# Attention: probabilities scaled on two engines and transposed by the identity

## The chip, the cores and the metric

The kernel runs on one core of a Trainium2 chip. A core has five engines that run side by side, each through its own queue of instructions in order: TensorE (PE in the profile; its weight loads are PEld), VectorE (DVE), ScalarE (ACT), GpSimd (POOL) and SyncE (SP), which issues the DMA transfers. Matrix products read SBUF and write PSUM, eight banks of 128 partitions by 512 float32 values. The metric is the device time of one execution in microseconds, the median of several.

## The reference, cut to what matters

The reference is a two-layer decoder trunk on 512 tokens of 1024 features in float32: a gated mixer, two gated feed-forward parts with a short convolution, per-layer embeddings, and, in the second layer, sliding-window attention with 16 heads of 64 features over 4 shared key and value heads. The change lies in the attention alone:

```python
scores = einsum('bnikgd,bnjkd->bnkgij', q, kblk) * (HEAD_DIM ** -0.5)
scores = scores - slopes * dist            # ALiBi
scores = where(valid, scores, -inf)        # this block of 128 keys and the one before
m = maximum(max(scores), sink)
e = exp(scores - m)
probs = e / (sum(e) + exp(sink - m))
out = einsum('bnkgij,bnjkd->bnikgd', probs, vblk)
out.reshape(B, S, 1024) @ w_o
```

## The kernel before, in words

Features lie on the 128 partitions and the 512 tokens along the free dimension. Every large product is made of three float32r products: weights and activations are each split into a rounded high part and a remainder (`wh`, `wl`; `xh`, `xl`), and high x high, high x low and low x high are added in PSUM (`mm3`, L162 to L170; `mm3t`, L172 to L181, for products with the tokens on the partitions). Weights stream in by DMA into raw buffers (`load`, L117, issued at L124), ScalarE casts the high part of each unit (L141) and VectorE subtracts for the low part (L142). The planned list of pieces is used in the order in which the layers need them. During the attention steps a single raw buffer is in use.

The attention (L622 to L720) takes 16 steps: four groups of four heads, and in each group four blocks of 128 tokens. The first block of a group sees 128 keys, the other three see 256. A step `i` passes through four functions, each written out for a different step in one pass of the loop: `scores(i)`, then filler work, `mix(i - 2)`, `turn(i - 1)` and `weights(i)`.

- `scores(i)`, L622: for each of the four heads, two products of queries and keys (L636, L637) into a half of a PSUM bank (tile `sc`). VectorE adds the position term, masks, writes the result to `pr` in SBUF and keeps the row's extreme in `neg` (L639). ScalarE takes the exponential in place and accumulates the sums `sm` (L644), and the exponential of the sink, `ds` (L648). `pr` has two buffers.
- `weights(i)`, L651: VectorE adds the sums to `ds` and takes the reciprocal (L654, L655), so that `ds` holds one factor per token and head. Then it builds `dg`, four 128 x 128 diagonal matrices with these factors (L657). `dg` has one buffer.
- `turn(i)`, L660: TensorE multiplies each 128 x 128 block of `pr` with its diagonal (L667). The block is the stationary operand, so the result in PSUM (tile `tr`) is the block transposed, with keys on the partitions, and scaled. `split` (L213) lets ScalarE write the rounded high part (L214) and VectorE the remainder (L215).
- `mix(i)`, L678: products with the values (L691) into `pv`, which ScalarE and VectorE split into the two parts of the attention output (`oh`, `ol`, L697 and L698).

The filler work of a step (`beside`, L593) is a piece of the projection of the next group's queries (tile `q`), of the values (`vv`) or, towards the end, of the output projection (`o`). Queries of groups 1 to 3 are scaled on VectorE (L529), split by ScalarE and VectorE (L540, L541) and moved by DMA from SP's queue into the two halves of the score operand (L544, L545).

A scheduler orders the instructions of each engine; `scores`, `turn` and `weights` stand under a higher priority, so that they are placed ahead of filler work that is ready at the same time. PSUM has eight banks, all shared by one pool.

Of the kernel before, what the change touches and what calls it, by code (L numbers as in the profile page):

```python
# [8 lines left out]
F32 = mybir.dt.float32  # L9
F32R = mybir.dt.float32r  # L10
AF = mybir.ActivationFunctionType
ALU = mybir.AluOpType

P = 128
# [11 lines left out]
GQ = HEADS // GROUPS  # L26
# [20 lines left out]
def tile_yoco(ctx: ExitStack, tc: tile.TileContext, t, out: bass.AP, out_b: bass.AP):  # L47
    nc = tc.nc
# [10 lines left out]
    def psum(name):  # L59
        return mmp.tile([P, S], F32, tag="mm", name=name)  # L60
# [144 lines left out]
    ident = const.tile([P, P], F32, name="ident")  # L205
# [7 lines left out]
    def split(src, hi, lo):  # L213
        nc.scalar.copy(hi, src)  # L214
        nc.vector.tensor_sub(lo, src, hi.bitcast(F32))  # L215
# [241 lines left out]
    for c in range(4):  # L457
# [4 lines left out]
        for j in range(2):  # L462
# [7 lines left out]
            for b in range(NC):  # L470
                nc.tensor.matmul(sp[:, b * P : (b + 1) * P], zv[b][:, m * P : (m + 1) * P], wsT[:, m, :],
                                 start=True, stop=True)
# [19 lines left out]
    at = ctx.enter_context(tc.tile_pool(name="at", bufs=1))  # L492
# [127 lines left out]
    live = {}  # L620
# [30 lines left out]
    def weights(i):  # L651

        pr, nk, sm, ds = live[i]
        nc.vector.tensor_add(ds, ds, sm)  # L654
        nc.vector.reciprocal(ds, ds)  # L655
        dg = at.tile([P, GQ, P], F32, tag="dg", name=f"dg{i}")
        nc.vector.tensor_mul(dg, ident.unsqueeze(1).to_broadcast([P, GQ, P]), ds.unsqueeze(2).to_broadcast([P, GQ, P]))  # L657
        live[i] = (pr, nk, dg)

    def turn(i):  # L660

        pr, nk, dg = live[i]
        pts = []
        for b in range(nk // P):
            tr = psum(f"tr{i}_{b}")
            for e in range(GQ):
                nc.tensor.matmul(tr[:, e * P : (e + 1) * P], pr[:, e, b * P : (b + 1) * P], dg[:, e, :],  # L667
                                 start=True, stop=True)
            q = state["pt"] = (state["pt"] + 1) % 3
            if q == 2:  # L670
                ph, pl = (ap.tile([P, S], F32R, tag=f"a{x}{SLOTS - 1}", name=f"p{x}{i}_{b}") for x in "hl")
            else:
                ph, pl = pts4[:, 2 * q, :], pts4[:, 2 * q + 1, :]
            split(tr, ph, pl)
            pts.append((ph, pl))
        live[i] = pts
# [27 lines left out]
    for i in range(last + 2):  # L704
        if i < last:
            with tc.high_priority():
                scores(i)
        fill(i)
        if i >= 2:
            mix(i - 2)  # L710
        if 0 <= i - 1 < last:
            with tc.high_priority():
                turn(i - 1)
        if i < last:
            with tc.high_priority():
                weights(i)
# [95 lines left out]
    for q in range(2):  # L812
        for c, ps in enumerate(turned):
            y = tp.tile([P, S], F32, tag=f"c{c}", name=f"y{c}_{q}")
            r = root[1][:, c : c + 1]
# [71 lines left out]
```

## Time and profile before

| | |
|---|---|
| median of 3 runs | 1176.94 us (1176.49 to 1177.97) |
| profiled execution | 1177.48 us, its span 1175.8 us |
| granted TensorE clock | 0.999 |
| PE busy | 1160.8 us, 99% |
| PEld busy | 989.0 us, 84% |
| DVE busy | 747.2 us, 64% |
| ACT busy | 521.0 us, 44% |
| POOL busy | 77.4 us, 7% |
| products with the diagonal (L667) | 224 instructions, from 605.4 to 713.2 us |
| diagonals (L657) | 16, 687 ns each |

The span runs from the first to the last instruction of the core. A row of a group names the line, the engine, the operation, the tile that is written and the tiles that are read, the partitions and elements, then how often it occurs, its busy time in total, the mean duration of one in ns, and the idle time of the engine ahead of it with what ended it. A row of the order in time has the start and the duration in us first. The durations of neighbouring products on TensorE overlap in these rows, because a product is shown from its start to the end of its pipeline; the distance between starts tells what one costs in a stream.

### The profile page before, as it was taken

Reading aid. Unit: us, or ns where it says so; the run is one execution under the profiler, and the core shown is the slowest. Engines: PE = TensorE matmul, PEld = TensorE weight load, DVE = VectorE, ACT = ScalarE, POOL = GpSimd, SP = SyncE. Lnnn points to the kernel's source line nnn. Section 1 sums busy time; section 2 is a strip of 40 time slices with the busy share of each in tenths; the row PEclk is TensorE's granted clock in tenths of the full one; section 3 lists DMA queues with packets and bytes.
Section 4 is the critical chain, followed back from the end, with each engine's and each line's share of the span. In section 5 each row is a group of like instructions: output and inputs, shape, how many; then the busy total and the mean of one; then the engine's idle time right before and its main releaser. Section 6 shows DMA issues by size and latency. Waiting matters only on the chain.

```text
span 1175.8 us, 14550 instructions
## 1 busy us (share of the span) xinstructions
PE 1160.8 (99%) x5830; PEld 989.0 (84%) x5830; DVE 747.2 (64%) x1159; ACT 521.0 (44%) x845; POOL 77.4 (7%) x87
## 2 busy tenths in 40 slices
PE   7999999999999999999999999999999999999997
PEld 7988888888888888888889888888888888888897
DVE  6365467763676377458877876577635773675665
ACT  5633444431344244545566665444313432345532
POOL 1000210000000000032100002100000000000221
PEclk9999999999999999999999999999999999999999
DMA  9232323322322333231243213322322233223302
GB/s 324 79 108 72 108 72 108 107 75 105 108 72 90 110 105 113 103 109 36 72 103 95 74 53 143 108 88 92 108 102 77 99 99 108 90 93 105 108 1 72
DMA packets 21570, 114.40 MB, mean 97 GB/s; under 512 B 2688, under 2 KB 4096, under 8 KB 11264
## 3 DMA queue, kind: packets, MB, share of 16 engines
q1 hardware_dynamic: 20672, 112.44, 28.3%
q8 instruction: 45, 0.74, 0.3%
q10 hardware_dynamic: 832, 1.05, 0.3%
q14 instruction: 21, 0.17, 0.0%
HBM read 107.19 MB, written 2.10 MB: 93 GB/s over the span
## 4 chain that ended last, share of the span: by engine, by line
PE 96%; DVE 1%; issue 1%; ACT 1%; DMA 0%; SPq 0%; POOLq 0%; POOL 0%; DVEq 0%; ACTq 0%
PE up L170 14%; PE up L168 14%; PE up L169 14%; PE d L169 8%; PE d L170 8%; PE d L168 8%; PE gate L169 2%; PE gate L168 2%; PE gate L170 2%; PE tr L667 2%; PE pv L691 1%; PE v L179 1%; PE v L180 1%; PE v L181 1%; PE o L170 1%; PE o L168 1%
## 5 line engine op out<-in xcount | busy, mean ns | idle before, releaser
L142 DVE TENSOR_TENSOR wl<-wraw,wh 128x1024 fp32r<-128x1024 f32 (+1 forms) x198 | 238.6, 1206 | 141.6 <-ACT wh L141 141.1
L141 ACT CAST wh<-wraw 128x1024 fp32r<-128x1024 f32 (+1 forms) x198 | 202.9, 1026 | 272.4 <-PE d L169 132.2
L168 PE MATMUL up<-nf10h,wh 128*128 128x512 f32 x352 | 137.1, 389 | 0.0
L168 PE MATMUL up<-nf00h,wh 128*128 128x512 f32 x352 | 137.1, 389 | 0.0
L170 PE MATMUL up<-nf00h,wl 128*128 128x512 f32 x352 | 137.0, 389 | 0.0
L170 PE MATMUL up<-nf10h,wl 128*128 128x512 f32 x352 | 137.0, 389 | 0.0
L169 PE MATMUL up<-nf00l,wh 128*128 128x512 f32 x352 | 136.9, 389 | 0.0
L169 PE MATMUL up<-nf10l,wh 128*128 128x512 f32 x352 | 136.9, 389 | 0.0
L168 PE MATMUL d<-ah,wh 128*128 128x512 f32 x352 | 136.9, 389 | 0.0
L169 PE MATMUL d<-al,wh 128*128 128x512 f32 x352 | 136.9, 389 | 0.0
L170 PE MATMUL d<-ah,wl 128*128 128x512 f32 x352 | 136.9, 389 | 0.0
L325 ACT ACTIVATE c<-hs,vec 128x512 f32<-128x512 f32 x88 | 71.3, 813 | 71.8 <-DVE hs L321 71.1
L326 DVE SCALAR_TENSOR_TENSOR c<-hs,vec,c 128x511 f32<-128x511 f32 x88 | 65.8, 748 | 34.2 <-ACT c L325 34.2
L301 DVE TENSOR_TENSOR h<-h,d 128x512 f32<-128x512 f32 x56 | 38.4, 686 | 73.7 <-PE d L170 73.7
L169 PEld LDWEIGHTS up<-nf00l,wh 128*128 128x128 f32 x352 | 66.1, 188 | 13.8
L168 PEld LDWEIGHTS up<-nf10h,wh 128*128 128x128 f32 x352 | 66.1, 188 | 13.8
L168 PEld LDWEIGHTS d<-ah,wh 128*128 128x128 f32 x352 | 66.1, 188 | 13.8
L169 PEld LDWEIGHTS d<-al,wh 128*128 128x128 f32 x352 | 66.1, 188 | 13.7
L169 PEld LDWEIGHTS up<-nf10l,wh 128*128 128x128 f32 x352 | 66.1, 188 | 13.7
L170 PEld LDWEIGHTS up<-nf00h,wl 128*128 128x128 f32 x352 | 66.1, 188 | 13.7
L168 PEld LDWEIGHTS up<-nf00h,wh 128*128 128x128 f32 x352 | 66.1, 188 | 13.7
L170 PEld LDWEIGHTS up<-nf10h,wl 128*128 128x128 f32 x352 | 66.1, 188 | 13.7
(291 smaller groups left out, 2163.8 us busy)
## 6 DMA issues: line engine op xcount, KB each, us to landing
wraw<-in_w_up SPq DMA_DIRECT2D x44, 1024.0 KB, 4.8
wraw<-in_w_down SPq DMA_DIRECT2D x16, 896.0 KB, 4.5
wraw<-in_w_down SPq DMA_DIRECT2D x8, 1024.0 KB, 4.8
wraw<-in_w_gate SPq DMA_DIRECT2D x8, 1024.0 KB, 4.8
wraw<-in_w_u SPq DMA_DIRECT2D x4, 1024.0 KB, 5.9
wraw<-in_w_out SPq DMA_DIRECT2D x4, 1024.0 KB, 5.3
wraw<-in_w_q SPq DMA_DIRECT2D x4, 1024.0 KB, 4.8
wraw<-in_w_o SPq DMA_DIRECT2D x4, 1024.0 KB, 5.0
```

Source lines behind the costliest of these rows:

```text
L141: nc.scalar.copy(wh[:, :n], src)
L142: nc.vector.tensor_sub(wl[:, :n], src, wh[:, :n].bitcast(F32))
L168: nc.tensor.matmul(ps, wh[:, a:b], xh, start=st, stop=False)
L169: nc.tensor.matmul(ps, wh[:, a:b], xl, start=False, stop=False)
L170: nc.tensor.matmul(ps, wl[:, a:b], xh, start=False, stop=en)
L179: nc.tensor.matmul(ps, xh[:, s], wh[:, a:b], start=st, stop=False)
L180: nc.tensor.matmul(ps, xl[:, s], wh[:, a:b], start=False, stop=False)
L181: nc.tensor.matmul(ps, xh[:, s], wl[:, a:b], start=False, stop=en)
L301: nc.vector.tensor_add(h[m], h[m], ps)
L325: nc.scalar.activation(c, hs, AF.Identity, bias=v("conv_b", l * 2 * NJ + col), scale=cw[2])
L326: nc.vector.scalar_tensor_tensor(c[:, 1:], hs[:, : S - 1], cw[1], c[:, 1:], op0=ALU.mult, op1=ALU.add)
L667: nc.tensor.matmul(tr[:, e * P : (e + 1) * P], pr[:, e, b * P : (b + 1) * P], dg[:, e, :], start=True, stop=True)
```

## The change

In `weights`, the diagonal matrices are gone. The factors are applied to the exponentials themselves, in place in `pr`: of the four heads, VectorE scales heads 0 and 2 and ScalarE heads 1 and 3, each over all keys of the step (128 or 256). In `turn`, the product with the diagonal becomes the transpose operation of TensorE, with the constant 128 x 128 identity as the other operand. `ident` exists in both kernels. The tile `dg` is no longer allocated. All else is the same text; the scheduler places the instructions of the attention steps anew.

```diff
         nc.vector.tensor_add(ds, ds, sm)
         nc.vector.reciprocal(ds, ds)
-        dg = at.tile([P, GQ, P], F32, tag="dg", name=f"dg{i}")
-        nc.vector.tensor_mul(dg, ident.unsqueeze(1).to_broadcast([P, GQ, P]), ds.unsqueeze(2).to_broadcast([P, GQ, P]))
-        live[i] = (pr, nk, dg)
+        for e in range(GQ):
+            a, r = pr[:, e, :nk], ds[:, e : e + 1]
+            if e in (1, 3):
+                nc.scalar.activation(a, a, AF.Copy, scale=r)
+            else:
+                nc.vector.tensor_scalar_mul(a, a, r)
+        live[i] = (pr, nk)
 
     def turn(i):
 
-        pr, nk, dg = live[i]
+        pr, nk = live[i]
         pts = []
         for b in range(nk // P):
             tr = psum(f"tr{i}_{b}")
             for e in range(GQ):
-                nc.tensor.matmul(tr[:, e * P : (e + 1) * P], pr[:, e, b * P : (b + 1) * P], dg[:, e, :],
-                                 start=True, stop=True)
+                nc.tensor.transpose(tr[:, e * P : (e + 1) * P], pr[:, e, b * P : (b + 1) * P], ident)
```

## The prediction

> **What bounds the kernel now.** I read the page first (engines, then the chain that ended last), then the busy time of each engine over the attention steps, then TensorE's order of instructions in a few of them, then the groups of instructions by shape.
>
> ```profile
> span 1175.8 us, 14550 instructions
> PE 1160.8 (99%) x5830; PEld 989.0 (84%) x5830; DVE 747.2 (64%) x1159; ACT 521.0 (44%) x845; POOL 77.4 (7%) x87
> ...
> PE 96%; DVE 1%; issue 1%; ACT 1%; DMA 0%; SPq 0%; POOLq 0%; POOL 0%; DVEq 0%; ACTq 0%
> ```
>
> TensorE carries 96% of the chain. A change is worth what it takes from TensorE's stream, less what it makes TensorE wait. The edit lies in the 16 attention steps, about 595 to 716 us. Busy time there, in stretches of four steps (columns: PE, PEld, DVE, ACT, POOL, granted clock, DMA share, GB/s):
>
> ```profile
> 606.00:633.04 27.04, 27.04 (x185) 24.62 (x184) 20.50 (x56) 16.15 (x45) 0.00 (x0) 1.00 0.42 118
> 633.04:660.10 27.06, 26.89 (x182) 24.00 (x180) 21.48 (x69) 17.58 (x56) 0.00 (x0) 1.00 0.28 79
> 660.10:687.18 27.08, 26.95 (x181) 24.05 (x180) 20.83 (x69) 18.47 (x56) 0.00 (x0) 1.00 0.29 79
> ```
>
> TensorE is full, VectorE at 76 to 79%, ScalarE at 60 to 68%. TensorE's own wait for VectorE in the whole stage is 0.2 us (scores for the read of their bank). So its instructions set the period, and the next limits are VectorE and ScalarE, some 20% below.
>
> The durations of single products overlap; what one costs is the distance between starts:
>
> ```profile
> 704.27 1.95 PE L667 MATMUL tr<-dg,pr 128*128 128x128 f32 x16
> 705.97 0.36 PE L691 MATMUL pv<-pl,vth 128*128 128x256 f32 x1
> 706.17 0.29 PE L691 MATMUL pv<-ph,vtl 128*128 128x256 f32 x1
> 706.29 0.28 PE L691 MATMUL pv<-ph,vth 128*128 128x256 f32 x1
> ...
> 1168.21 0.36 PE L767 MATMUL fms<-mean,facc 128*128 128x1 f32 x2
> 1168.44 0.36 PE L767 MATMUL fms<-mean,fsq 128*128 128x1 f32 x2
> 1168.66 1.14 PE L804 MATMUL ht<-dgain,h 128*128 128x128 f32 x8
> ```
>
> From 704.27 to 706.17 stand 16 products and one pv, which elsewhere takes 0.12 (706.17 to 706.29): 1.78 us for 16, 0.111 each. The code issues 8 there, so one f32 product runs as two instructions of 0.111, 0.222 us together. The f32 products with one moving column take as long (1168.21 to 1168.44, two in 0.23): at this size the weight load sets the pace, not the 128 columns.
>
> ```profile
> L667 PE MATMUL tr<-dg,pr 128*128 128x128 f32 x224 | 31.1, 275 | 0.0
> L657 DVE TENSOR_TENSOR dg<-ident,ds 128x512 f32<-128x512 f32 x16 | 11.0, 687 | 0.1
> L454 DVE TENSOR_SCALAR zv<-zv,vrt 128x1024 f32<-128x1024 f32 x4 | 2.7, 749 | 1.1 <-POOL vrt L270 1.1
> L772 DVE TENSOR_SCALAR dgain<-ident,vec 128x128 f32<-128x128 f32 x8 | 1.7, 280 | 3.1 <-PE pin L169 3.1
> L644 ACT ACTIVATE pr<-pr,neg 128x256 f32<-128x256 f32 x48 | 24.3, 506 | 10.7 <-DVE neg L639 10.6
> L644 ACT ACTIVATE pr<-pr,neg 128x128 f32<-128x128 f32 x16 | 6.4, 400 | 5.5 <-DVE neg L639 5.4
> L570 ACT ACTIVATE vth<-vv,n1rt 128x256 fp32r<-128x256 f32 x4 | 1.9, 474 | 1.7 <-PE vv L181 1.5
> L697 ACT CAST oh<-pv 128x128 fp32r<-128x128 f32 x32 | 8.2, 257 | 3.6 <-DVE ol L698 1.9 <-PE pv L691 1.2
> ```
>
> **The change, part by part.**
>
> *TensorE.* 224 instructions are 112 products with the diagonal (12 steps of 8, 4 of 4), 24.9 us of the stream. The compiled program of the changed kernel holds 5718 matmuls and as many weight loads, 112 fewer than the 5830 of the page: a transpose is one pair, not two. No row shows a transpose. Bounds of its cost: no f32 instruction here, not even one of one column, follows another in less than 0.111; from above, what both passes take now, 0.222, or, if neighbours do not overlap, the 0.275 that one instruction lasts. I take 0.111, because probabilities are still the 128-column f32 weights whose load sets that pace. Gain 112 x 0.111 = **12.4 us**, all on the path; a stretch of four steps holds 28 products and shrinks from 27.1 to 24.0 us.
>
> The Trainium skill ("TensorE: Matmul & The Clock Gate", Terms) says that the transpose mode is four times faster for f32. By that rule a product would go from 0.222 to 0.056 and the gain would be 18.6 us; the one-column rows above speak for the load's 0.111 as the floor instead (rival D).
>
> *VectorE.* Loses 16 diagonals, 11.0 us. Gains two scalings a step, 24 of 128x256 and 8 of 128x128. No row has 128x256; between 280 ns (128 columns) and 749 (1024), both VectorE scalings of SBUF, a straight line gives 347 (bounds: 280, and 476 of the score read of 256 columns). 24 x 0.347 + 8 x 0.280 = 10.6 us. Net -0.4 (-2.0 to +2.7); its stretch stays near 21 us of 24.0, 86 to 89%. Off the path. The diagonal's single buffer also goes, so the scaling no longer waits for the previous step's products; it stands straight behind the reciprocal in nearly every step.
>
> *ScalarE.* Gains the other 32 scalings. For 256 columns the nearest row is the scaled copy of vth, 474 ns (bounds: 417, a Square of 256 columns, and 506, the exponential); for 128 columns 257 to 400, I take 330. 24 x 0.474 + 8 x 0.330 = 14.0 us, 3.5 a stretch: 21.1 and 22.0 us of 24.0, 88 to 92%. No further table load: seven in both programs.
>
> *The new wait.* ScalarE's scalings wait for VectorE's sum and reciprocal: at step 1 the sink's exponential starts at 602.44 and the reciprocal ends at 603.04, so 0.4 us after the exponential. In the changed order nothing stands between the two on ScalarE at steps 1, 2 and 12; elsewhere a copy of values or pv, or other casts do. Behind the waiting instruction are queued the casts of the transposed blocks, the query copies and the next exponentials; their readers are VectorE, SP and TensorE. TensorE needs a step's scaled block only a step later: from the end of a diagonal to its first product are 2.7 us or more, except 0.75 and 1.0 at steps 13 and 14. VectorE's half now comes earlier than the diagonal did, ScalarE's half about 1 us after the reciprocal, so this hides, with up to 0.5 us at step 14 where the cover is thin.
>
> *What is late next.* Queries of group 3 are first read by the second pair of scores of step 12. Their last half leaves VectorE after the last score read of step 11:
>
> ```profile
> 678.39 0.69 DVE L541 TENSOR_TENSOR qf<-qf,qhi 128x512 fp32r<-128x512 f32 x1
> ...
> 679.11 1.10 SPq L545 DMA_DIRECT2D q<-qf  x2
> ...
> q<-qf SPq DMA_DIRECT2D x12, 128.0 KB, 2.3
> ```
>
> The scores of step 11 end with the pair at 677.55, and the copy lands at 679.11 + 2.3 = 681.4, 3.9 us later; now TensorE comes for it at 681.8. In the changed order 1 pv, 5 transposes, 2 scores, 3 transposes, 10 pv, 2 scores and 1 pv stand between: 12 x 0.12 + 8 x 0.111 + three pairs of scores at 0.24 (the one of 677.55 with them) = 3.1 us. So TensorE waits 0.8 us there (0 to 1.3). At step 8 the same count gives 4.2 us, no wait. SP: the second and third w_o load now stand ahead of the copies of a group's second query projection instead of among them; they wait for the same casts as before, and the row of 2.3 was taken with such a load (1 MB, 5.0 us to landing) around it, so nothing (0 to 1 us). POOL is not touched.
>
> *Sum.* 1177.48 (profiled execution: span 1175.8 and 1.7 around it) - 12.4 + 0.8 (queries) + 0.7 (score reads: TensorE's next start is 0.3 late now at 655.80 in step 8 and at 682.89 in step 12; I let both double and round up for step 14) = 1166.6. The profiled execution lies 0.5 above the median of 1176.94, so **1166.0 us**.
>
> **Rivals.**
>
> *A. ScalarE or VectorE becomes the bound.* With the dearer prices ScalarE's stretch is 18.5 + 6 x 0.506 + 2 x 0.400 = 22.3, and with 0.6 us of wait for the reciprocal in each of four steps 24.7, over TensorE's 24.0. It decides once scalings and waits pass 5.5 us a stretch. Four stretches lose 0.7 each, and as much again through VectorE behind ScalarE's casts: 5.6 us, about 1171; 1169 to 1174.5. For it: 90% on two in-order engines that wait for each other. Against: one step of slack.
>
> *B. The transpose keeps the pace of both passes.* At 0.222 nothing is saved, ScalarE has 27 us for its 22: 1177, no change. For it: the 0.111 of the pass itself could be hidden under the load. Against: half the loads are gone.
>
> *C. Slower: transposes do not overlap.* Each takes the 275 ns of the L667 row: 112 x 0.275 = 30.8 against 24.9, +5.9, about 1183. It decides above 0.222 a product. For it: no row shows a transpose beside other products. Against: every f32 and fp32r product here overlaps its neighbour.
>
> The Trainium skill ("TensorE: Matmul & The Clock Gate", Part 4) gives about 275 ns for a transpose within one kernel.
>
> *D. A transpose takes a quarter of the f32 product*, 0.056, load included: 112 x 0.166 = 18.6, less 1.5 of waits, 1160. Against: no weight load here follows another so closely.
>
> *E. The clock falls around the transposes.* Half clock for 1 us of work in each of 16 steps costs 16 us: 1166 + 16 = 1182 or more. Against: the granted clock is 1.00 in all stretches, and transposes would fill 0.9 of some 6 us a step. The same Part 4 of the Trainium skill's "TensorE: Matmul & The Clock Gate" says that transposes do not count as busy for the clock gate; no run here shows it.
>
> **How the numbers follow.** Forecast (1163.5 to 1168.5) 0.66, A 0.10, B 0.09, C 0.10, D 0.04, E 0.01. Faster: forecast, A, D, 0.80. 0.2% is 2.4 us, about what a measurement of this kernel can tell from no change: B splits into same 0.07 and slower 0.02; with C and E slower is 0.13. The range takes in D and A: 1159.5 to 1174.5, 0.80.
>
> **What would show it.** TensorE's tr group: 112 instructions, starts 0.111 apart (B: 0.222, C: 0.275, D: 0.056). A stretch of four steps near 24.4 us. ScalarE's scalings near 0.47, VectorE's near 0.35. A wait for the query copy before the second pair of scores in step 12. The stages outside unchanged to 0.5 us. I am wrong if the distance between transposes is not 0.111, or if TensorE's waits for score reads and casts pass 3 us in the stage.

## The result, and the profile after

The changed kernel takes 1166.47 us (median of 4 runs, 1165.95 to 1167.04), the kernel before on the same chip 1176.99 us (4 runs, 1176.49 to 1177.97): a ratio of 0.991 with a 95% interval of 0.9893 to 0.9927. Forecast were 1166.0 us and a gain of 0.9%. The profiled execution of the changed kernel took 1167.04 us, with a span of 1165.3.

The page of the changed kernel, the span, the engines and the chain that ended last:

```profile
span 1165.3 us, 14362 instructions
PE 1147.8 (98%) x5718; PEld 975.7 (84%) x5718; DVE 745.3 (64%) x1175; ACT 532.5 (46%) x877; POOL 77.6 (7%) x87
...
PE 95%; DVE 2%; DMA 1%; issue 1%; ACT 1%; SPq 0%; POOLq 0%; POOL 0%; DVEq 0%; ACTq 0%
```

TensorE still carries the chain. From the first scores product to the first product of the FFN behind the attention the stage takes 140.14 us (593.32 to 733.46) and took 150.33 (593.38 to 743.72). That is 10.19 us of the 10.44 by which the spans differ. From there to TensorE's last product it takes 425.8 us in both.

The busy time of the engines in stretches of four steps of the changed kernel (columns: stretch, its length, PE, PEld, DVE, ACT, POOL, granted clock, DMA share, GB/s):

```profile
605.41:630.24 24.83, 24.77 (x165) 22.34 (x163) 19.88 (x59) 18.21 (x50) 0.00 (x0) 1.00 0.43 128
630.24:655.25 25.01, 23.62 (x154) 20.88 (x152) 20.21 (x70) 19.54 (x61) 0.00 (x0) 1.00 0.32 85
655.25:680.27 25.02, 23.76 (x154) 20.92 (x152) 21.21 (x77) 21.02 (x66) 0.00 (x0) 1.00 0.32 84
```

27.04 to 27.08 us have become 24.8 to 25.0, and TensorE is no longer full: 1.4 and 1.3 us of the last two stretches are idle. The clock is 1.00. VectorE is at 80 to 85%, ScalarE at 73 to 84%.

TensorE's order in time at a block of transposes of the changed kernel:

```profile
695.82 1.03 PE L671 MATMUL tr<-ident,pr 128*128 128x128 f32 x8
696.61 0.36 PE L694 MATMUL pv<-pl,vth 128*128 128x256 f32 x1
696.81 0.28 PE L694 MATMUL pv<-ph,vtl 128*128 128x256 f32 x1
```

From 695.82 to 696.81 stand eight transposes and one pv of 0.12: 0.87 us for eight, 0.109 each. Eight products with the diagonal took twice that.

The groups of instructions of the changed kernel's attention, by shape (busy us, mean ns of one, idle before):

```profile
L671 PE MATMUL tr<-ident,pr 128*128 128x128 f32 x112 | 18.3, 273 | 0.0
L659 ACT ACTIVATE pr<-pr,ds 128x256 f32<-128x256 f32 x24 | 11.3, 504 | 2.8 <-DVE ds L655 2.8
L659 ACT ACTIVATE pr<-pr,ds 128x128 f32<-128x128 f32 x8 | 2.8, 397 | 1.0 <-DVE ds L655 1.0
L661 DVE TENSOR_SCALAR pr<-pr,ds 128x256 f32<-128x256 f32 x24 | 7.4, 349 | 0.2
L661 DVE TENSOR_SCALAR pr<-pr,ds 128x128 f32<-128x128 f32 x8 | 1.9, 284 | 0.1
```

A transpose lasts 273 ns, as an f32 pass did; only the distance between starts tells its price. Its weight load lasts 140 ns, against 192 before.

What TensorE waited for in the attention from 595 us on (us in total, times, longest), then the chain at the longest wait (start us, us, what), of the changed kernel:

```profile
PE sc L636 <- DMA q<-qf: 2.6, 2, 1.4
PE sc L636 <- DVE neg L639: 0.2, 1, 0.2
```

```profile
646.83 0.48 DVE pr L639
647.31 0.01 DVE neg L639
647.31 0.60 DVE qf L541
647.92 0.03 DVE ds L647
647.95 4.00 DMA q<-qf
651.95 0.14 issue
652.09 0.30 PE sc L636
```

At step 8 the scores of the third head, the first in the step's second PSUM bank, need the second half of group 2's queries. Their last part leaves VectorE behind the last score read of step 7, and the copy then takes 4.00 us. Counted against the normal distance of instructions, TensorE loses 1.53 us there and 1.47 at step 12 (2.96 us for the copy). In a second profiled execution of the same kernel these were 0.99 and 1.09.

The 10.19 us, from sums of the distances between starts: transposes 21.84 to 8.97 (-12.87); waits of more than 0.12 us, 2.27 to 5.19 (+2.92); all other products together -0.24.

### The profile page after: what moved, and what is told of

The parts are those of the page before. It is cut to its first block, busy times and chain, and to the rows that moved or that the text cites. A ratio compares the mean times of both kernels' runs of the same rounds, so it can differ in the third digit from the quotient of the medians.

```text
span 1165.3 us, 14362 instructions
## 1 busy us (share of the span) xinstructions
PE 1147.8 (98%) x5718; PEld 975.7 (84%) x5718; DVE 745.3 (64%) x1175; ACT 532.5 (46%) x877; POOL 77.6 (7%) x87
## 4 chain that ended last, share of the span: by engine, by line
PE 95%; DVE 2%; DMA 1%; issue 1%; ACT 1%; SPq 0%; POOLq 0%; POOL 0%; DVEq 0%; ACTq 0%
PE up L168 14%; PE up L170 14%; PE up L169 14%; PE d L170 8%; PE d L169 8%; PE d L168 8%; PE gate L169 2%; PE gate L168 2%; PE gate L170 2%; PE v L179 1%; PE pv L694 1%; PE v L180 1%; PE v L181 1%; PE o L168 1%; PE o L169 1%; PE o L170 1%
## 5 line engine op out<-in xcount | busy, mean ns | idle before, releaser
L142 DVE TENSOR_TENSOR wl<-wraw,wh 128x1024 fp32r<-128x1024 f32 (+1 forms) x198 | 238.8, 1206 | 141.7 <-ACT wh L141 141.4
L170 PEld LDWEIGHTS d<-ah,wl 128*128 128x128 f32 x352 | 66.1, 188 | 13.7
```

The costliest lines, as they stand in the source:

```text
L142: nc.vector.tensor_sub(wl[:, :n], src, wh[:, :n].bitcast(F32))
L170: nc.tensor.matmul(ps, wl[:, a:b], xh, start=False, stop=en)
```

## The experiments

Theory: TensorE sets the period, a transpose costs it 0.11 us, and what is missing from the gain is the wait for query copies. Rivals: part of the gain comes from elsewhere in the edit (the diagonals gone from VectorE, the shorter chain); VectorE or ScalarE is the new bound; the missing part is not to be had.

### One part alone: scaled probabilities, but the plain product

```diff
-                nc.tensor.transpose(tr[:, e * P : (e + 1) * P], pr[:, e, b * P : (b + 1) * P], ident)
+                nc.tensor.matmul(tr[:, e * P : (e + 1) * P], pr[:, e, b * P : (b + 1) * P], ident, start=True, stop=True)
```

> The scaling on ScalarE and VectorE stays as in the changed kernel, but the block is multiplied with the identity as a plain f32 product in place of the transpose. Theory (the gain is the second pass of the products): 224 tr instructions 0.111 us apart come back, 112 x 0.111 = 12.4 us more on TensorE, and with that much more work between them the query copies are covered again, so the two waits of 1.5 us before scores go: 1166.5 + 12.4 - 2 to 3, that is 1176 to 1178. Rival (the gain came from the diagonals that VectorE no longer builds, or from the new order): 1166 to 1170.

Measured: 1175.93 us, ratio to the kernel before 0.9987 (0.9978 to 0.9997). The group of transposes:

```profile
L671 PE MATMUL tr<-ident,pr 128*128 128x128 f32 x224 | 31.1, 275 | 0.0
```

The 224 instructions are back, 21.75 us of the stream by their starts, and TensorE is full (53.91 of 54.00 us from 605 to 659). The time lies just under the range of the theory. Against the kernel before on the same chip (1177.63 us) scaling on two engines in place of the diagonals is worth little by itself: 0.4 to 2.6 us by the interval of the ratio, 0.90 us in the attention stage of the two profiled executions. The rest comes from the transposes' single pass, the only line of the program in which this kernel differs from the changed one.

### The price in place: every transpose twice

```diff
-                nc.tensor.transpose(tr[:, e * P : (e + 1) * P], pr[:, e, b * P : (b + 1) * P], ident)
+                for _ in range(2):
+                    nc.tensor.transpose(tr[:, e * P : (e + 1) * P], pr[:, e, b * P : (b + 1) * P], ident)
```

> The changed kernel with each of the 112 transposes issued twice, the second over the first. If a transpose costs TensorE its distance to the next (0.109 to 0.111 us in the changed kernel's trace), 112 more add 12.2 to 12.4 us of work, of which the two waits for query copies (1.53 and 1.47 us) may cover 1 to 3: 1175.5 to 1179 us. If a transpose costs its own duration of 0.27 us wherever it stands: +30 us, 1197. If a second one with the same data were nearly free: 1167 to 1169.

Measured: 1176.68 us, ratio 0.9994 (0.9984 to 1.0003), as slow as before. The transposes' sum by starts went from 8.97 to 21.09 us: 12.12 for 112, 0.108 each. The price of 0.27 us and the price of nothing fall. The waits shrank by 1.6 us, since a longer stream reaches the queries later; the copies cost TensorE this (us in total, times, longest):

```profile
PE sc L636 <- DMA q<-qf: 1.8, 2, 0.9
```

With 112 more of them the clock stays at 1.00.

### No scaling at all

```diff
-            if e in (1, 3):
-                nc.scalar.activation(a, a, AF.Copy, scale=r)
-            else:
-                nc.vector.tensor_scalar_mul(a, a, r)
```

> Leaves out the scaling by the reciprocal of the sum (the probabilities stay unnormalised); the transposes stay. Theory (the 64 scalings lie beside TensorE's work): between 1164 and 1167; what can go is only the part of the two query waits that comes from casts queued behind scalings on ScalarE. Rival (ScalarE or VectorE limits the changed kernel): 1163 or less, and TensorE's stretch of four steps falls from 25.0 us to 24.0.

Measured: 1167.82 us (1167.27 to 1170.14), ratio 0.9924 (0.9909 to 0.9938): no faster than with all 64 scalings, a little above the range of the theory and far from that of the rival. Their time and their wait for the reciprocal were hidden. The waits for copies stay (2.3 us in all). The profiled execution, at 1170.14 the longest, shows one thing more, in stretches around the copy's wait at step 12:

```profile
672.00:677.50 5.50, 4.16 (x31) 3.64 (x30) 4.22 (x17) 3.17 (x13) 0.00 (x0) 1.00 0.61 226
677.50:680.90 3.40, 3.40 (x11) 2.69 (x10) 0.97 (x7) 1.08 (x5) 0.00 (x0) 0.52 0.00 0
```

For 3.4 us behind the wait the granted clock is 0.52, which costs half of these, 1.7 us. I come back to it below.

### VectorE as the bound: all scalings on it

```diff
-            if e in (1, 3):
+            if False:
```

> The changed kernel with all four scalings of a step on VectorE. In each four steps VectorE gets 8 x 0.349 = 2.8 us more (20.2 to 21.2 -> 23.0 to 24.0 of 25.0 us) and ScalarE loses 8 x 0.504 = 4.0. If TensorE still sets the pace: 1166 to 1168.5 us. If VectorE is near its limit (rival A of the prediction, on the other engine), its score reads come late, as with the diagonals in one pass, where 6.0 us of waits came of it: 1169 to 1174.

Measured: 1166.51 us, ratio 0.9907 (0.9893 to 0.9922), the same as the changed kernel. VectorE takes 32 more scalings without a loss: it is not the bound.

### The old way in one pass: diagonals, but float32r

```diff
-        pr = mp.tile([P, GQ, 2 * P], F32, tag=f"m{4 + i % 2}", name=f"pr{i}")
+        pr = mp.tile([P, GQ, 2 * P], F32R, tag=f"m{4 + i % 2}", name=f"pr{i}")
...
-        dg = at.tile([P, GQ, P], F32, tag="dg", name=f"dg{i}")
+        dg = at.tile([P, GQ, P], F32R, tag="dg", name=f"dg{i}")
```

> The kernel before with products with the diagonal in float32r in place of f32: probabilities, diagonals and the scores that are written to pr are rounded to float32r, and no scaling is added. Theory (what counts is one weight load and one pass per block instead of two, not the transpose operation): 112 tr instructions 0.11 to 0.12 apart, 1164 to 1168. Rival (the transpose mode has a pace of its own that a plain product of one pass doesn't reach): 1171 or more.

Measured: 1172.58 us, ratio 0.996 (0.9946 to 0.9975): my theory of the pass alone was 4 us too fast here. The group and the waits of TensorE:

```profile
L667 PE MATMUL tr<-dg,pr 128*128 128x128 f32 x112 | 17.3, 258 | 0.0
...
PE sc L636 <- DVE neg L639: 6.0, 10, 0.8
```

112 single passes, about as cheap as transposes: without its waits the attention stage takes 135.5 us here and 134.95 in the changed kernel. With its waits (10.24 us against 5.19) it takes 145.74 against 140.14, and the new ones are ten waits of the scores for VectorE's score reads. VectorE's amount of work is not the reason: its diagonals are 11.0 us, and the experiment before gave it 17.9 us of scalings for nothing. Nor does a diagonal (L657) stand ahead of the reads (L639) that come late. VectorE's order ahead of the first long wait, which ends at 633.50:

```profile
631.75 0.69 DVE L541 TENSOR_TENSOR qf<-qf,qhi 128x512 fp32r<-128x512 f32 x1 [0.69 <-ACT qhi L540]
632.36 0.68 DVE L215 TENSOR_TENSOR pts<-tr,pts 128x512 fp32r<-128x512 f32 x1
632.97 0.47 DVE L639 CUSTOM_DVE_ANT_0 pr<-far,sc,nsink 128x256 fp32r<-128x256 f32 x1
...
633.36 0.69 DVE L657 TENSOR_TENSOR dg<-ident,ds 128x512 fp32r<-128x512 f32 x1
```

The read stands behind the subtraction of a transposed block (L215), and VectorE had sat idle before that until ScalarE's cast of the queries was done. The order is the same at all ten waits: the instruction just ahead of the read is the subtraction of a block or of a weight piece (L142), and the diagonal follows. So the rest of the edit does have a part in the gain: once the passes are single, the new kernel's stage is 5.6 us shorter than the old order's. What part of this is owed to the scalings, to the diagonal tile that is gone, or to the scheduler's new order of all engines, no run separates.

### Queries first

```diff
-            qs[g] += queries(box["qp"], g, j)
+            with tc.high_priority():
+                qs[g] += queries(box["qp"], g, j)
```

> The changed kernel with the scaling, splitting and copying of the queries placed under the higher priority, so that VectorE subtracts their low part ahead of three of the four score reads of the step before they are needed. Theory (the two waits of 1.5 us of TensorE before scores in steps 8 and 12 are the copies of the queries, which leave VectorE too late): both waits fall under 0.3 us, 1163.0 to 1164.5. Rival (the waits only move to the score reads, because VectorE has no room): 1165.5 to 1167.

Measured: 1167.55 us, ratio 0.9917 (0.9902 to 0.9932), no gain and above both ranges. The theory had the wrong half of the path. SyncE's queue and the chain around step 8, of this kernel:

```profile
644.82 0.54 SPq L124 DMA_DIRECT2D wraw<-in_w_o  x1
645.63 1.10 SPq L545 DMA_DIRECT2D q<-qf  x2
```

```profile
645.00 0.60 DVE qf L541
645.61 0.03 DVE pr L662
645.63 5.43 DMA q<-qf
```

VectorE's half is ready at 645.6, 2.3 us earlier than in the changed kernel, but the 1 MB load of w_o has gone out 0.8 us ahead of the copy, and the copy takes 5.43 us. It lands at 651.07, against 651.95. New theory: the copy is late because of that load, by the order of one queue or because the DMA engines are full.

### The copies on another queue

With queries first, and:

```diff
-            nc.sync.dma_start(q[me, :].bitcast(F32), hi[me, :])
-            nc.sync.dma_start(q[it, :].bitcast(F32), qf[me, :])
+            nc.gpsimd.dma_start(q[me, :].bitcast(F32), hi[me, :])
+            nc.gpsimd.dma_start(q[it, :].bitcast(F32), qf[me, :])
```

> The changed kernel with the later queries computed as early as in the run before (queries first) and their copies issued by GpSimd instead of SyncE, so that they are not in the queue behind the 1 MB load of w_o. If the copies were late because that one queue works in order, they land within about 3 us of VectorE's subtraction, the waits of TensorE at steps 8 and 12 go, and the time is 1163 to 1165 us. If the 16 DMA engines are simply full of the load (or GpSimd issues late), the copies still take 4 us and more and the time stays at 1166.5 to 1168.

Measured: 1176.43 us, ratio 0.9992 (0.9982 to 1.0001), far above both ranges: the whole gain is lost. The profiled execution, at 1174.87 us, is the fastest of ten. The chain at step 8, then TensorE's waits, then stretches around step 8 (columns as above):

```profile
646.75 5.28 DMA q<-qf
```

```profile
PE sc L637 <- DMA q<-qf: 6.3, 2, 3.2
```

```profile
648.90:652.16 3.26, 0.18 (x2) 0.03 (x1) 0.71 (x2) 0.58 (x2) 0.00 (x0) 1.00 0.72 224
652.16:655.40 3.24, 3.24 (x20) 3.18 (x21) 2.18 (x14) 2.06 (x9) 0.00 (x0) 0.76 0.02 5
655.40:659.63 4.23, 4.23 (x21) 3.51 (x19) 2.43 (x11) 2.55 (x12) 0.00 (x0) 0.78 0.00 0
```

The copies take as long from their own queue. GpSimd's issuing is not what makes them late: it takes 0.52 us for a copy, and the copy issued at 644.74, ahead of the load, lands after 2.2 us, while the next, issued at 645.25 and 0.04 us behind the load, needs 6.4. The 0.88 MB that the DMA engines moved from 646.65 to 649.70 all belonged to the load. So it is the DMA engines' load and not the order on SyncE. The Trainium skill says the same ("DMA: Bandwidth & Descriptors", Issuing engines are not separate DMA queues): whoever issues them, transfers run on the same 16 engines. It also has them interleave there, which the copies behind this load did not do. The price is larger than the two waits of 3.2 and 3.4 us: 1.7 us after the end of the first and 0.4 us after the end of the second the granted clock falls to 0.50 for 3.4 us, and a q product takes 0.43 instead of 0.23.

### No copies

With queries first, and the halves cast and subtracted straight into the query tiles, as group 0 does it:

```diff
-        if g == 0:
+        if True:
```

> Queries first, and for all groups the halves are written by ScalarE and VectorE straight into the query tiles, as the kernel does for group 0: 24 DMA copies of 128 KB go, six casts of 0.62 us and six subtractions of 0.69 us come, 3.7 and 4.1 us in the whole attention, on engines that were busy 19 to 21 of each 25 us. If the copies' landing is what TensorE waited for at steps 8 and 12, both waits go and the time is 1163 to 1165 us. If VectorE is so full that its 4.1 us delay the score reads, 1166 to 1169. It would beat both kernels in the first case.

Measured: 1166.09 us, ratio 0.9905 (0.989 to 0.992). Stretches of four steps, and TensorE's waits:

```profile
631.20:655.26 24.06, 23.86 (x154) 20.89 (x151) 21.97 (x76) 20.63 (x65) 0.00 (x0) 1.00 0.13 45
655.26:679.35 24.09, 23.92 (x152) 20.93 (x152) 21.55 (x75) 20.71 (x67) 0.00 (x0) 1.00 0.13 44
```

```profile
PE sc L637 <- DVE neg L640: 1.1, 4, 0.5
```

The waits for copies are gone and the stretches are the 24.0 us of the prediction. Yet the whole is not measurably faster than the changed kernel, which in a later series gave 1165.95 us and 0.9906:

> The changed kernel itself, for a comparison on one chip: 1166.5 us within 0.7.

Against that series' profile (groups of four steps 31.38, 24.48, 24.76) this kernel has 32.22, 24.06, 24.09: 1.1 us won, 0.84 given back in the first group, where scores now wait 0.62 us for a score read after 617.91 and 0.44 after 626.36. Ahead of the first of these reads stands one of the added subtractions (L536), ahead of the second only the usual ones (L142, L215), so that the added work is the cause of both is not shown.

The same without moving the queries:

> The changed kernel with the query halves written straight into the tiles by ScalarE and VectorE (no DMA copies), but the queries left at their old place in the order. If it is the copies' landing that costs TensorE 1.5 us at steps 8 and 12, removing them is enough: the scores then wait for VectorE's subtractions after the last score read of steps 7 and 11 (0.69 us each, up to 1.4 us for two): waits of 0 to 0.8 us there, 1165 to 1166.5 us. If the order is what matters, waits of 1.5 us and more for VectorE take the place of those for the copies: 1167 to 1169.

Measured: 1166.71 us, ratio 0.991 (0.9892 to 0.9928). TensorE waits 0.53 and 0.52 us for VectorE's subtraction at steps 8 and 12 in place of 1.53 and 1.47 for the copy, and here too the first group is longer, 31.99. Just above the range of the one theory, below that of the other, and no different from the changed kernel.

### ScalarE as the bound: all scalings on it

Queries first, no copies, and:

```diff
-            if e in (1, 3):
+            if True:
```

> Queries first, no copies, and all four scalings of a step on ScalarE: for each four steps VectorE loses 8 x 0.349 = 2.8 us (22 -> 19 of 24 us) and ScalarE gets 4.0 us (20.8 -> 24.8 of 24 us). If VectorE's fullness makes the last waits for score reads (1.1 us with queries first and no copies), they go: 1165 to 1165.7 us. If ScalarE has become the bound (rival A of the prediction), stretches of four steps rise above 24.1 us, to 24.8 and more, with waits of TensorE for transposes' inputs or split probabilities: 1167 to 1171.

Measured: 1169.42 us, ratio 0.9935 (0.9917 to 0.9953). Stretches, and the place where most is lost:

```profile
630.90:655.05 24.15, 24.01 (x151) 20.80 (x150) 20.13 (x67) 22.84 (x73) 0.00 (x0) 1.00 0.14 46
655.05:680.01 24.96, 24.73 (x154) 21.07 (x154) 19.73 (x66) 23.74 (x74) 0.00 (x0) 1.00 0.10 32
```

```profile
694.58 1.64 PE L672 MATMUL tr<-ident,pr 128*128 128x128 f32 x8 [0.78 <-ACT pr L660]
```

ScalarE at 95% gives the last transposes their input one scaling at a time: they start 0.94 us late and stand 0.2 us apart. Rival A is real at this load, with the casts of all queries on ScalarE too: it costs some 3 us against the same kernel with half of the scalings on each engine (1166.09).

### The subtractions on GpSimd

Queries first, no copies, and:

```diff
-                nc.vector.tensor_sub(q[it, :], qf[me, :], q[me, :].bitcast(F32))
+                (nc.vector if g == 0 else nc.gpsimd).tensor_sub(q[it, :], qf[me, :], q[me, :].bitcast(F32))
```

> Queries first, no copies, and the subtractions of groups 1 to 3 on GpSimd, which does nothing in these stretches: VectorE loses 12 x 0.69 = 8.2 us over the attention, and GpSimd needs 12 times some 1.5 us (its 128x512 sums take 1.37 to 1.55 us), 3 us for a projection, with some 5 us between the queries and the scores that need them. If VectorE's fullness makes the last waits for score reads: 1164.5 to 1165.5 us, which would be the best so far. If GpSimd's subtractions come too late: waits of 1 us and more at steps 4, 8 and 12 and 1167 to 1170.

Measured: 1167.56 us, ratio 0.9919 (0.9903 to 0.9935): no faster than with VectorE's own subtractions (1166.09). It lies in the second range, but not for the reason given there: the queries are in time, VectorE's score reads are not:

```profile
PE sc L637 <- DVE neg L640: 3.6, 6, 1.3
```

VectorE and GpSimd ahead of the longest of these waits, in order of time:

```profile
643.21 2.70 POOL L536 TENSOR_TENSOR q<-qf,q 64x512 fp32r<-64x512 f32 x2 [9.41 <-ACT q L535]
...
643.71 2.35 DVE L662 TENSOR_SCALAR pr<-pr,ds 128x256 f32<-128x256 f32 x2
...
646.58 0.47 DVE L640 CUSTOM_DVE_ANT_0 pr<-far,sc,nsink 128x256 f32<-128x256 f32 x1
```

Two scalings that take 0.349 us each elsewhere take 0.98 and 1.45 while GpSimd subtracts.

## Why the prediction was right, and which terms were not

*Transposes, 12.4 us.* Right. 0.109 apart in the trace, 0.108 by doubling them, -12.87 us in the stage by starts. Rivals B (0.222), C (0.275) and D (0.056) fall by this distance. By the rule of the Trainium skill that I weighed ("TensorE: Matmul & The Clock Gate", Terms: four times faster for f32) it would have been 0.056; the trace shows half of an f32 product and no more. Its 275 ns (Part 4, of a bf16 block) agrees with how long one lasts here, 273, which is not what it costs. The reason that the prediction gave for the price is not confirmed: the weight load of a transpose lasts 140 ns and not 192, and the distance stays, so that the load sets it is not shown. Nor is 0.111 a floor for all starts, as the prediction has it: in the kernel before, the first two one-column products at 578.08 start 0.026 apart, and only the weight loads all keep at least 0.108.

*VectorE and ScalarE.* VectorE's prices (347 and 280 forecast, 349 and 284 measured) were right, ScalarE's low (474 and 330 against 504 and 397). Still ScalarE came out at 78 and 84% of the last two stretches and not 88 to 92%: the page has it 11.5 us busier, not 15 (24 x 0.504 + 8 x 0.397), because its instructions overlap their neighbours by some 0.1 us, and because the stretches were longer than 24.0. Rival A did not happen, and the two kernels with all scalings on one engine show how far off it was: at no price on VectorE, at some 3 us on ScalarE with all query casts there as well.

*The new wait for the reciprocal.* Right to count as hidden: ScalarE waited 3.8 us for it in all, and leaving the scaling out altogether won nothing.

*Query copies, 0.8 us at step 12 and none at step 8.* This is the term that failed. The cover was counted rightly: from the last scores of the step before to TensorE's turn it is 3.2 us at step 12 (3.1 forecast) and 4.2 at step 8 (4.2), and the copy goes out 1.56 us behind those scores, as forecast. With the 2.3 us of the prediction the waits would by these starts have been 0.8 and none. The landing took 2.96 and 4.00 us, and they were 1.47 and 1.53 (1.09 and 0.99 in the second execution). The wrong term is that of SyncE's order, "nothing (0 to 1 us)". SyncE's queue around step 12, of the kernel before and then of the changed kernel:

```profile
674.70 1.10 SPq L544 DMA_DIRECT2D q<-qhi  x2
675.89 0.55 SPq L124 DMA_DIRECT2D wraw<-in_w_o  x1
679.11 1.10 SPq L545 DMA_DIRECT2D q<-qf  x2
```

```profile
669.12 0.33 SPq L124 DMA_DIRECT2D wraw<-in_w_o  x1
670.14 1.10 SPq L544 DMA_DIRECT2D q<-qhi  x2
673.33 1.10 SPq L545 DMA_DIRECT2D q<-qf  x2
```

In the kernel before only VectorE's half (`qf`) went out behind the load, 3.2 us later, and it landed in 2.52 us, 0.5 us after the load. In the changed kernel ScalarE's half (`qhi`) is behind the load too: the load lands at 674.69, ScalarE's two copies at 675.19 and 675.75, VectorE's only then, at 676.29. At step 8 the load and a copy of ScalarE's stand ahead as well, and VectorE's copy lands 1.9 us after the load (1.25 in the second execution); why that is more than at step 12, where two copies stand ahead, stays open.

*Score reads, 0.7 us.* Too much, by the waits for them: the four of 0.17 to 0.32 us of before went, five of 0.15 to 0.22 came.

*The sum.* Waits grew by 2.92 us and not by 1.5, transposes gave 12.87 and not 12.4, the other products of the stage 0.24 and the rest of the span 0.25: 1166.6 forecast for the profiled execution, 1167.04 measured. The errors have opposite signs, so that the time came this close is in part luck. The stretch of "near 24.4 us" was 24.8 to 25.0; 24.06 without copies.

*The clock (E).* 1.00 in every stretch of the changed kernel, and with twice the transposes.

## What to carry to other kernels

Price a TensorE instruction by the distance between starts, not by its length, and an f32 product with an identity or a diagonal as two: a transpose is one. When the bounding engine's stream becomes shorter, go through the transfers that end just before it needs them, and count their landing anew with all that the new order issues ahead of them: the 2.3 and 2.5 us that the same copies took in the old order became 4.0 and 3.0. A wait that can be removed is worth only what the next engine leaves: here none of three ways around two waits of 1.5 us made the kernel measurably faster.

## What the runs showed of the hardware that I had not expected

- **An idle TensorE costs twice.** After idle gaps of 3.24 and 3.39 us (copies on GpSimd's queue) the granted clock fell to 0.50 for about 3.4 us. The Trainium skill ("TensorE: Matmul & The Clock Gate", Part 1) has half the clock after an idle window of about 3.4 us that runs freely. The runs agree on size and length, but in one execution of the kernel without scaling it fell to 0.50 after a wait of only 1.3 us, also for 3.4 us, while those of 1.5 us in the changed kernel did nothing. Why that one did is open.
- **GpSimd stops VectorE's scaling.** A scaling of 0.349 us became 0.98 and 1.45 beside GpSimd's subtraction of 1.3 us. The Trainium skill ("SBUF — State Buffer", Who interferes with whom) describes a port pair that either of the two holds for a whole instruction; VectorE's end times fit that, each shortly after one of GpSimd's (643.21 + 1.33 = 644.54, scaling ends 644.69).
- **A small copy waits behind a large load, whichever engine issues it.** A copy of 128 KB landed 2.2 us after GpSimd issued it ahead of a 1 MB load, and 6.4 us when it was issued 0.04 us behind the load; on SyncE's queue it took 5.43 us where the load had gone out 0.8 us before.
- **The weight load of a transpose is shorter** (140 ns against 192) without any effect on the distance: 0.109 against 0.111.
